# A hybrid encoder layer in half products: new figures in the planner that sets each engine's order

## The chip, the core and the metric

The kernel runs on one core of a Trainium2 chip, in one launch. The metric is the time of that launch on the device, in microseconds (us). Differences here are some tenths of a per cent.

A core has engines that run side by side, each with a queue of its own that it works through in order: TensorE (PE, matmuls; PEld is its loading of weights), VectorE (DVE), ScalarE (ACT), GpSimd (POOL), and SyncE (SP), which here issues all loads and stores. An instruction that needs another engine's result waits for it at the head of its queue, and everything behind it waits too.

## The reference

One layer over 2048 tokens of 1024 features, batch 1, float32:

```python
xn = rms_norm(x, mix_norm_g)
aq, ak, av, mq, mk, mv, mo, i, f, ga, gm = split(xn @ w_in)
A = chunk_band_attention(aq, ak, av, rel_bias)         # 8 heads, chunks of 64, own and 8 before
q, k = split(silu(causal_conv(concat(mq, mk))))
M = sigmoid(mo) * rms_norm(mlstm_chunkwise(q, k, mv, i + b_i, f + b_f))   # 4 heads
y = sigmoid(ga) * (A @ w_att_proj) + sigmoid(gm) * (M @ w_mlstm_proj)
x = x + y @ w_out
x = x + square(relu(rms_norm(x, ffn_norm_g) @ w_up)) @ w_down
out = rms_norm(x, final_norm_g)
```

## The kernel before

**The work.** Each float32 product is made of three matmuls on operands split into a high and a low part (`r` tiles for activations, `wsp` tiles for weights, both float32r; the low part is the value less the high part). ACT casts the high part (L682 for weights, L1651 for activations), DVE subtracts for the low part (L684, L1656, L1658). Large products are blocked 2 by 2 and computed with seven half products in place of eight, so DVE also adds and subtracts blocks before and after. A matmul takes 128x128 weights and 512 columns, into one of eight PSUM banks.

**The stages that matter here.** The layer runs as input projection, attention and mLSTM with further projections (L850) beside them, then from about 1950 us the projections of the mixers' results (`project_quads`, L1255), `w_out`, and the feed-forward part.

- Before `project_quads`, the mixers' results lie in DRAM as `mix0` to `mix3` and `mixa3`. SP loads blocks of them (L1193, L1137, L1138), DVE forms the sums of blocks (L1204, L1140), ACT and DVE split them (L1651, L1656).
- In `project_quads` the weights come as tiles that were split earlier: SP loads them, 1 MB each, from `wsplit29_0` to `wsplit29_6` in DRAM into one of three `wsp` buffers (L587). Each half product fills a bank. ACT copies a bank to an `sc` or `ctx` buffer (L1293), or DVE adds it to such a copy (L1302). Then DVE multiplies by the gate, which SP loaded (L1278), at L1313, and adds the two mixers at L1321.
- Around 1147 and 1208 us, L850's projections go on beside the mLSTM: ACT copies banks (L2286), applies the gates' tanh (L2427) and the convolution's activations (L2458, L2467), DVE the convolution's sums (L2465, L2469) and L2294.

**What sets the order.** The program is first written by some hundred cooperating threads. Then the class `Order` takes all instructions, works out which depends on which (`graph`), and lists them anew for each engine:

- `cost` gives each instruction a duration from its shape, `transfer` one to each DMA, `lag` the delay between an instruction and one that depends on it.
- `due` gives each instruction the time by which it should be done: PE's instructions in the order of the program, summed up; all others backwards from these, less their durations, their lags and, for SP, `FAR`.
- `run` plays the engines forward. On DVE, ACT and SP the instruction with the earliest due time among those whose inputs would be there goes next; on PE the one that comes first in the program. For SP it counts a queue and at most `FLY` = 8 transfers in flight.
- The resulting order on each engine is fixed in the program by dependences without a wait.

So the figures in `Order` decide no duration on the chip, only which instruction stands ahead of which. 12690 matmuls, 3873 DVE, 2458 ACT and 2325 SP instructions are ordered so.

Of the kernel before, what the change touches and what calls it, by code (L numbers as in the profile page):

```python
# [24 lines left out]
F32 = mybir.dt.float32  # L25
# [203 lines left out]
class Order:  # L229
# [1 line left out]

    MARGIN = dict(PE=600.0, Activation=100.0, DVE=100.0, Pool=100.0, SP=2500.0)
    WAKE = dict(PE=43.0, DVE=23.0, Activation=23.0, Pool=69.0, SP=16.0)
    REACH, LAND, FAR, FLY = 1400.0, 1100.0, 2500.0, 8

    def __init__(self, tc):
        self.tc = tc
# [33 lines left out]
    def cost(self, i, e):  # L271
        ins, outs = self.operands(i.ins), self.operands(i.outs)
        n = max(self.count(a) for a in ins + outs)
        bank = any(a.tensor.name.startswith("bank") for a in ins + outs)
        if e == "PE":
            return max(110.0, 13.7 + self.count(outs[0]) / 2.4)
        if e == "SP":
            return 365.0
        if e == "Activation":
            return (75 if bank else 93) + 0.84 * n + (190 if len(outs) > 1 else 0)  # L280
        if e == "Pool":
            return 1200.0 if n <= 8 else 80 + 1.27 * n
        if n <= 4:
            return 155.0
        two = sum(self.count(a) > 4 for a in ins) > 1
        return 60 + (1.13 if two or bank else 0.66) * n + (80 if len(outs) > 1 else 0)

    def transfer(self, i):
        a, b = self.operands((i.outs[0], i.ins[0]))
# [29 lines left out]
    def lag(self, j, k):  # L319
        e, to = self.eng[j], self.eng[k]  # L320
        if e == to != "SP":
            return 0.0
        t = self.WAKE[to] + (0.0 if e == "SP" else 13.0)
        return t + (0.0 if e != "PE" else 175.0 if self.dur[j] >= 140.0 else 130.0)

    def due(self):
# [55 lines left out]
class Layer:  # L382
    LATE, LATE_SPLIT = 3000.0, 2500.0
# [2664 lines left out]
```

## Time and profile before

| what | value |
| --- | --- |
| median of 3 runs | 2767.21 us (2766.9 to 2769.65) |
| the profiled execution, its time | 2767.92 us |
| its span in the profile | 2766.1 us |
| mean granted clock of TensorE | 0.998 |
| DVE, busy | 2100.4 us |
| ACT, busy | 1509.2 us |
| DMA queue of SP | 701.60 MB, 76.6% of 16 engines' span |

The profiled execution's time is 1.8 us more than its span: what lies before the first and behind the last instruction. Each long matmul (128x512) starts 0.227 us behind the one before it, while the trace gives it a duration of about 0.39, since matmuls overlap. Idle time is therefore read from the rows of waits, not from a sum of durations. In a timeline a row is: start, length, engine, line, operation, and in brackets the idle time ahead of it with the instruction that ended it. In the rows names stand without buffer numbers.

### The profile page before, as it was taken

What the parts mean: (1) busy time and instruction counts of PE and PEld (TensorE: products, weight loads), DVE (VectorE), ACT (ScalarE), POOL (GpSimd) and SP (SyncE); (2) the same over time, 40 slices, a digit from 0 to 9 for tenths busy, and PEclk for the clock granted to TensorE, in tenths of its full rate; (3) what the DMA queues carried; (4) which work ended last, traced back from release to release, by engine and by line L of the source; (5) the groups of instructions that cost most, each with busy time, mean ns of one, the idle gap of its engine ahead of it and who ended that gap; (6) DMA issues with size and microseconds to landing.
All of it is one profiled execution on the core that took longest, in us unless ns stands there. A gap on an engine that the chain in (4) does not pass through costs nothing.

```text
span 2766.1 us, 38799 instructions
## 1 busy us (share of the span) xinstructions
PE 2744.5 (99%) x13006; PEld 2282.9 (83%) x13006; DVE 2100.4 (76%) x3873; ACT 1509.2 (55%) x2665; POOL 51.7 (2%) x101
## 2 busy tenths in 40 slices
PE   9999999999999999999999999999999999999999
PEld 7888888888778888777888888888778888888888
DVE  7796799777996866876677788889898755555566
ACT  5664576644454545585456566566335655554444
POOL 0010001000000000000000000000000000000000
PEclk9999999999999999999999999999999999999999
DMA  8968849889756588489899999887967667676564
GB/s 286 286 220 263 238 157 309 299 272 333 265 194 232 196 285 313 136 280 317 293 313 311 308 272 269 263 247 242 330 232 245 216 217 263 236 247 216 195 222 162
DMA packets 339416, 704.08 MB, mean 255 GB/s; under 512 B 37992, under 2 KB 68880, under 8 KB 337424
## 3 DMA queue, kind: packets, MB, share of 16 engines
q1 hardware_dynamic: 339072, 701.60, 76.6%
q8 instruction: 102, 1.67, 0.2%
q14 instruction: 98, 0.80, 0.1%
q10 hardware_dynamic: 144, 0.01, 0.0%
HBM read 483.60 MB, written 217.86 MB: 254 GB/s over the span
## 4 chain that ended last, share of the span: by engine, by line
PE 92%; DVE 4%; DMA 2%; ACT 1%; issue 1%; SPq 0%; DVEq 0%; ACTq 0%
PE bank L850 42%; PE bank L765 11%; PE bank L767 11%; PE bank L766 11%; PE bank L881 3%; PE bank L1842 2%; PE bank L1255 2%; PE bank L1815 2%; PE bank L1873 2%; DVE ctx L2465 1%; DVE wsp L684 1%; PE bank L2128 1%; PE bank L2129 1%; PE bank L2127 1%; PE bank L2113 0%
## 5 line engine op out<-in xcount | busy, mean ns | idle before, releaser
L850 PE MATMUL bank<-r,wsp 128*128 128x512 f32 x5544 | 1268.7, 391 | 6.6 <-ACT ctx L2286 3.3
L850 PEld LDWEIGHTS bank<-r,wsp 128*128 128x128 f32 x5544 | 1039.8, 188 | 227.4 <-ACT ctx L2286 4.7
L684 DVE TENSOR_TENSOR wsp<-wraw,wsp 128x1024 fp32r<-128x1024 f32 x442 | 540.6, 1223 | 347.9 <-ACT wsp L682 338.4
L682 ACT CAST wsp<-wraw 128x1024 fp32r<-128x1024 f32 x442 | 464.9, 1052 | 529.0 <-PE bank L766 211.6
L765 PE MATMUL bank<-r,wsp 128*128 128x512 f32 x1328 | 530.3, 400 | 0.5 <-ACT ctx L2106 0.5
L767 PE MATMUL bank<-r,wsp 128*128 128x512 f32 x1328 | 519.9, 392 | 0.0
L766 PE MATMUL bank<-r,wsp 128*128 128x512 f32 x1328 | 519.4, 391 | 0.0
L767 PEld LDWEIGHTS bank<-r,wsp 128*128 128x128 f32 x1328 | 249.6, 188 | 52.7
L765 PEld LDWEIGHTS bank<-r,wsp 128*128 128x128 f32 x1328 | 249.8, 188 | 46.2 <-ACT ctx L2106 0.9
L766 PEld LDWEIGHTS bank<-r,wsp 128*128 128x128 f32 x1328 | 250.2, 188 | 44.2
L2294 DVE TENSOR_TENSOR ctx<-bank,ctx 128x512 f32<-128x512 f32 x186 | 127.5, 688 | 98.7 <-PE bank L850 96.5
L1656 DVE TENSOR_TENSOR r<-r 128x512 fp32r<-128x512 f32 x251 | 165.6, 687 | 9.6 <-ACT r L1651 9.4
L1651 ACT CAST r<-r 128x512 fp32r<-128x512 f32 x251 | 149.4, 622 | 28.2 <-DMA r<-u 23.5
L2286 ACT COPY ctx<-bank 128x512 f32<-128x512 f32 x186 | 107.7, 582 | 78.7 <-PE bank L850 61.1
L1857 ACT ACTIVATE sc<-sc,scs 128x640 f32<-128x640 f32 (+4 forms) x128 | 97.4, 762 | 67.2 <-DVE scs L1854 61.7
L1878 DVE TENSOR_TENSOR r<-bank,r 128x512 fp32r<-128x512 f32 (+1 forms) x168 | 97.0, 597 | 19.5 <-ACT r L1876 18.9
L1876 ACT CAST r<-bank 128x512 fp32r<-128x512 f32 (+1 forms) x168 | 81.9, 517 | 51.6 <-PE bank L1873 45.9
L1848 DVE CUSTOM_DVE_ANT_0 sc<-bank,bias 128x320 f32<-128x320 f32 (+3 forms) x240 | 103.7, 463 | 5.6 <-PE bank L1842 4.8
L2625 ACT ACTIVATE ctx<-ctx 128x512 f32<-128x512 f32 x96 | 60.5, 630 | 83.6 <-DVE ctx L2294 83.5
L1815 PE MATMUL bank<-r,r 128*128 128x512 f32 x336 | 94.9, 363 | 0.0
L701 DVE TENSOR_TENSOR wraw<-wraw,wraw 128x1024 f32<-128x1024 f32 x76 | 92.7, 1223 | 1.7
L1255 PE MATMUL bank<-r,wsp 128*128 128x512 f32 x336 | 81.0, 403 | 7.3 <-DVE tmp L1313 2.9
(295 smaller groups left out, 2987.3 us busy)
## 6 DMA issues: line engine op xcount, KB each, us to landing
wraw<-in_wf SPq DMA_DIRECT2D x178, 512.0 KB, 4.7
wraw<-wsum SPq DMA_DIRECT2D x136, 512.0 KB, 4.2
r<-u SPq DMA_DIRECT2D x224, 256.0 KB, 3.9
wraw<-in_w SPq DMA_DIRECT2D x71, 512.0 KB, 5.1
ctx<-in_wf SPq DMA_DIRECT2D x128, 256.0 KB, 5.2
u<-ctx SPq DMA_DIRECT2D x128, 256.0 KB, 3.5
wsum<-ctx SPq DMA_DIRECT2D x112, 256.0 KB, 4.4
u<-tmp SPq DMA_DIRECT2D x96, 256.0 KB, 3.9
```

What stands on the lines that cost most here:

```text
L682: nc.scalar.copy(w[:, 0], raw)
L684: nc.vector.tensor_sub(w[:, 1], raw, w[:, 0].bitcast(F32))
L765: mm(ps, lh, rh, start=first, stop=False)
L766: mm(ps, lh, rl, start=False, stop=False)
L767: mm(ps, ll, rh, start=False, stop=last)
L850: mm(ps, wv[:, x, k, n], a[:, y], start=new and k == 0 and x == y == 0, stop=k == 3 and x == 1, skip_group_check=True)
L1255: mm(ps, wv[:, y, x, k, n], a[:, z], start=m < 3 and k == y == z == 0, stop=k == 1 and y == 1, skip_group_check=True)
L1651: self.nc.scalar.copy(dst[:, 0], src)
L1656: self.nc.vector.tensor_sub(dst[:, 1], src, dst[:, 0].bitcast(F32))
L1815: nc.tensor.matmul(acc[:, :, c0:c0 + w], st, sl[:, :, o:o + w], start=n == 0, stop=n == total - 1)
L2286: nc.scalar.copy(t[:, o:o + 512], ps)
L2294: nc.vector.tensor_add(t[:, o:o + 512], ps, t[:, o:o + 512])
```

## The change

The change gives `Order` other figures. No instruction is added or left out, and nothing is computed differently.

- A column or a further input counts by the number of inputs: ACT is 92 ns longer for each input beside the first, DVE 62 ns longer with more than two (before: ACT 190 and DVE 80 where there was a second output).
- A matmul on plain float32 that isn't a transpose counts double.
- An instruction that depends on the one before it on the same engine waits `AGAIN` ns (before: 0); results of ACT and DVE reach other engines `LATE` ns later.
- `FAR`, by which SP's transfers are due ahead of their use, goes from 2500 to 5000 ns.

```diff
-    REACH, LAND, FAR, FLY = 1400.0, 1100.0, 2500.0, 8
+    AGAIN = dict(PE=0.0, Activation=125.0, DVE=85.0, Pool=60.0)
+    LATE = dict(PE=0.0, Activation=98.0, DVE=50.0, Pool=0.0)
+    REACH, LAND, FAR, FLY = 1400.0, 1100.0, 5000.0, 8
...
         if e == "PE":
-            return max(110.0, 13.7 + self.count(outs[0]) / 2.4)
+            plain = ins[0].dtype == F32 and not i.is_transpose
+            return max(110.0, 13.7 + self.count(outs[0]) / 2.4) * (2.0 if plain else 1.0)
...
-            return (75 if bank else 93) + 0.84 * n + (190 if len(outs) > 1 else 0)
+            return (75 if bank else 93) + 0.84 * n + 92 * (len(ins) - 1)
...
-        return 60 + (1.13 if two or bank else 0.66) * n + (80 if len(outs) > 1 else 0)
+        return 60 + (1.13 if two or bank else 0.66) * n + (62 if len(ins) > 2 else 0)
...
         if e == to != "SP":
-            return 0.0
-        t = self.WAKE[to] + (0.0 if e == "SP" else 13.0)
+            return self.AGAIN[e]
+        t = self.WAKE[to] + (0.0 if e == "SP" else 13.0 + self.LATE[e])
```

In the new order 707 of the 12690 matmuls stand in another place (by at most 24), 2430 of DVE's 3873 instructions, 982 of ACT's 2458 and 1254 of SP's 2325. From here on, lines of code behind the changed ones have numbers that are 3 higher in the changed kernel (L1313 is L1316); the text uses those of before.

Three places are shown, in the order of before and then of the changed kernel.

**DVE at about 2004 to 2017 us, in `project_quads`.** L1313 multiplies a bank, or its copy in `sc`, by the gate; L1302 adds a bank to a copy. The instruction on `tmp2_108` and `sc3_104` frees `sc3`, which ACT's next copy (L1293) of bank 6 writes. Before:

```order
L1313 SCALAR_TENSOR_TENSOR ctx3_115<-ctx3_115,bank5_133 128x512
L1302 TENSOR_TENSOR sc0_98<-bank2_130,sc0_98 128x512
L1313 SCALAR_TENSOR_TENSOR ctx4_116<-ctx4_116,sc0_98 128x512
L1313 SCALAR_TENSOR_TENSOR tmp5_111<-tmp5_111,bank1_129 128x512
L1321 TENSOR_TENSOR ctx1_113<-ctx1_113,tmp5_111 128x512
L1302 TENSOR_TENSOR sc2_102<-bank5_133,sc2_102 128x512
L1313 SCALAR_TENSOR_TENSOR ctx15_127<-ctx15_127,sc2_102 128x512
L1302 TENSOR_TENSOR sc1_100<-bank1_129,sc1_100 128x512
L1313 SCALAR_TENSOR_TENSOR tmp4_110<-tmp4_110,sc1_100 128x512
L1313 SCALAR_TENSOR_TENSOR tmp2_108<-tmp2_108,sc3_104 128x512
```

and in the changed kernel:

```order
L1316 SCALAR_TENSOR_TENSOR ctx3_115<-ctx3_115,bank5_133 128x512
L1316 SCALAR_TENSOR_TENSOR tmp2_108<-tmp2_108,sc3_104 128x512
L1324 TENSOR_TENSOR ctx13_125<-ctx13_125,tmp2_108 128x512
L1316 SCALAR_TENSOR_TENSOR tmp5_111<-tmp5_111,bank1_129 128x512
L1324 TENSOR_TENSOR ctx1_113<-ctx1_113,tmp5_111 128x512
L1305 TENSOR_TENSOR sc0_98<-bank2_130,sc0_98 128x512
L1316 SCALAR_TENSOR_TENSOR ctx4_116<-ctx4_116,sc0_98 128x512
```

The instruction on `tmp2` and the sum behind it moved eight places up, to directly behind the one on `ctx3`. On PE, the six matmuls into bank 6 that wait for the copy moved 23 places up, ahead of three groups of six and five more matmuls. A second instruction on `tmp2`, later in this stretch, moved six places up.

**SP at about 1965 to 1977 us, ahead of `project_quads`.** Here `mix2`, `mix3` and `mixa3` are the mixers' results, `gate2` and `gate3` the gates, `wsplit29` the weights, and `fin` a store. Before:

```order
L587 DMA wsp2_63<-wsplit29_1 128x2048
L1278 DMA ctx10_122<-gate2 128x512
L1193 DMA tmp3_109<-mix2 128x512
L1193 DMA tmp4_110<-mix3 128x512
L2547 DMA fin0<-ctx9_121 128x512
L2547 DMA fin1<-ctx0_112 128x512
L587 DMA wsp0_61<-wsplit29_0 128x2048
L1193 DMA ctx6_118<-mix3 128x512
L1137 DMA tmp2_108<-mixa3 64x512
L1138 DMA tmp5_111<-mixa3 64x512
L1193 DMA tmp0_106<-mix3 128x512
```

and in the changed kernel:

```order
L1196 DMA tmp3_109<-mix2 128x512
L1196 DMA tmp4_110<-mix3 128x512
L2550 DMA fin0<-ctx9_121 128x512
L644 DMA wraw1_65<-in_wf 128x1024
L1196 DMA ctx6_118<-mix3 128x512
L1140 DMA tmp2_108<-mixa3 64x512
L1141 DMA tmp5_111<-mixa3 64x512
L1196 DMA tmp0_106<-mix3 128x512
L590 DMA wsp2_63<-wsplit29_1 128x2048
L1281 DMA ctx10_122<-gate2 128x512
```

The loads of `mix` and `mixa` and one store now stand ahead of both weight loads; `wsplit29_1` and the load of `gate2` moved seven places down, as did `wsplit29_0`, which now stands six rows behind `wsplit29_1`. On DVE, the sums of these blocks (L1204) and what follows from them moved ahead of the bank sums of L1302 by 11 or 12 places.

**ACT at about 1142 to 1148 us.** L2286 copies bank 6 to `ctx8`; L2427 works on a result of DVE. Before:

```order
L682 CAST wsp1_62<-wraw3_67 128x1024
L2286 COPY ctx2_114<-bank2_130 128x512
L2458 ACTIVATE ctx0_112<-ctx15_127,cvw_143 128x512
L2427 ACTIVATE ctx12_124<-ctx12_124 128x512
L2286 COPY ctx8_120<-bank6_134 128x512
L2467 ACTIVATE ctx15_127<-ctx0_112 128x512
L682 CAST wsp2_63<-wraw0_64 128x1024
```

and in the changed kernel:

```order
L2289 COPY ctx8_120<-bank6_134 128x512
L2430 ACTIVATE ctx12_124<-ctx12_124 128x512
L685 CAST wsp2_63<-wraw0_64 128x1024
L2470 ACTIVATE ctx15_127<-ctx0_112 128x512
L2430 ACTIVATE ctx10_122<-ctx10_122 128x512
```

The copy of bank 6 moved ahead of the activation on `ctx12`; the weights' cast moved ahead of L2467.

## The prediction

> **What bounds the kernel now.** I read the page's busy times first, then what TensorE waited for, then the windows of 100 us to place these waits. All rows are of the one profiled execution; times are us.
>
> ```profile
> PE 2744.5 (99%) x13006; PEld 2282.9 (83%) x13006; DVE 2100.4 (76%) x3873; ACT 1509.2 (55%) x2665; POOL 51.7 (2%) x101
> PE 92%; DVE 4%; DMA 2%; ACT 1%; issue 1%; SPq 0%; DVEq 0%; ACTq 0%
> ```
>
> TensorE is busy for 2744.5 of a span of 2766.1 and carries 92% of the chain that ended last. The change removes no matmul, so only the 21.6 us in which PE is not busy, and whatever makes matmuls longer, can move. About 1.0 of the 21.6 is the start (the row of L441 below, which stays). The rows of PE's waits say what else there is (waited for, total us, times, longest):
>
> ```profile
> PE bank L850 <- ACT ctx L2286: 3.3, 2, 1.9
> PE bank L1255 <- DVE tmp L1313: 2.9, 2, 2.1
> PE bank L1255 <- ACT r L1651: 2.0, 1, 2.0
> PE bank L1255 <- ACT sc L1293: 1.9, 1, 1.9
> PE bank L850 <- ACT r L1651: 1.7, 1, 1.7
> PE bank L850 <- DVE r L1658: 1.1, 2, 0.5
> PE bank L441 <- DVE ones L438: 1.0, 1, 1.0
> PE bank L1972 <- DVE cum L1968: 0.6, 2, 0.3
> ```
>
> The five largest rows add up to 11.8 us, in seven waits. Two stretches hold most of them, 1900 to 2100, where DVE is busy for 89% (columns: length, then busy time of PE, PEld, DVE, ACT, POOL, granted clock of PE, DMA share, GB/s):
>
> ```profile
> 1200.00:1300.00 100.00, 96.72 (x421) 78.34 (x420) 73.11 (x96) 61.49 (x93) 0.00 (x0) 1.00 0.90 313
> 1900.00:2000.00 100.00, 97.44 (x451) 80.62 (x450) 89.12 (x170) 48.86 (x88) 0.00 (x0) 0.98 0.83 276
> 2000.00:2100.00 100.00, 95.28 (x411) 77.78 (x410) 89.30 (x135) 34.46 (x54) 0.00 (x0) 0.98 0.68 236
> ```
>
> The clock of 0.98 in these two rows is a second cost. Behind some stalls PE runs at half clock:
>
> ```profile
> 1148.40:1151.80 3.40, 3.40 (x9) 2.67 (x9) 1.85 (x3) 1.74 (x4) 0.00 (x0) 0.51 0.62 224
> 1991.60:1995.00 3.40, 3.40 (x8) 2.72 (x9) 3.40 (x6) 1.17 (x2) 0.00 (x0) 0.51 0.76 309
> 2015.40:2018.80 3.40, 3.40 (x10) 2.63 (x9) 2.57 (x4) 0.00 (x0) 0.00 (x0) 0.51 0.56 113
> 2023.10:2026.50 3.40, 3.40 (x15) 2.81 (x16) 3.30 (x6) 0.39 (x1) 0.00 (x0) 1.00 0.75 214
> ```
>
> The last row is the same length at full clock: 15 matmuls, or 3.40 / 15 = 0.227 each. The other three did 9, 8 and 10, so the dips cost 6, 7 and 5 matmuls: 1.4, 1.6 and 1.1 us.
>
> The TensorE page of the Trainium skill ("TensorE: Matmul & The Clock Gate", section "What's actually happening") says that the clock is halved after at least one idle window of about 3.4 us. The trace disagrees on the length, since no wait above is over 2.1 us and three are followed by a dip. Taken strictly, the rule would give these dips a cause other than the stalls; that is the third rival.
>
> **The change part by part.** Nothing is computed differently; the tables order each engine's instructions anew. So no duration changes, and a term is a wait that goes or comes. I give no price to the tables themselves. I compare the two orders at each stall, and take the times from the trace of before.
>
> *A. The quads' later columns (2004 to 2026).* PE's rows, with the idle time in brackets, then DVE's and ACT's:
>
> ```profile
> 2010.05 2.79 PE L1255 MATMUL bank<-r,wsp 128*128 128x512 f32 x11 [0.75 <-DVE tmp L1313]
> 2014.70 6.23 PE L1255 MATMUL bank<-r,wsp 128*128 128x512 f32 x19 [1.86 <-ACT sc L1293]
> 2023.04 3.26 PE L1255 MATMUL bank<-r,wsp 128*128 128x512 f32 x13 [2.11 <-DVE tmp L1313]
> ```
> ```profile
> 2005.26 0.69 DVE L1313 SCALAR_TENSOR_TENSOR ctx<-ctx,bank 128x512 f32<-128x512 f32 x1 [0.67 <-PE bank L1255]
> 2007.98 0.69 DVE L1302 TENSOR_TENSOR sc<-bank,sc 128x512 f32<-128x512 f32 x1 [2.03 <-PE bank L1255]
> 2012.68 1.29 DVE L1313 SCALAR_TENSOR_TENSOR tmp<-tmp,sc 128x512 f32<-128x512 f32 x2
> 2022.30 0.68 DVE L1313 SCALAR_TENSOR_TENSOR tmp<-tmp,bank 128x512 f32<-128x512 f32 x1
> 2014.07 0.58 ACT L1293 COPY sc<-bank 128x512 f32<-128x512 f32 x1 [10.93 <-DVE tmp L1313]
> ```
>
> DVE's second instruction at 2012.68 (2013.3) frees the buffer that ACT's copy at 2014.07 needs, and the copy frees the bank that PE waits for until 2014.70. It stands behind eight instructions, of which the first waits 2.03 for PE. In the new order it is directly behind the one at 2005.26, where DVE is idle until 2007.98. It would end near 2006.9, and the copy 0.6 later, near 2007.5. The instruction of 2010.05's wait then ends by 2008.4, before PE asks at 2009.3 (2010.05 - 0.75). The one at 2022.30, for which PE waits 2.11, moves 6 up, 6 x 0.65 = 3.9 us. So the three waits go: 0.75 + 1.86 + 2.11 + the dip of 1.1 = 5.8. What is late next is the copy again: PE's group behind it is moved up too, by 23 matmuls, and asks at about 2006.6 (2009.3 less the two groups of six that it now precedes, 12 x 0.227 = 2.7). It would wait some 1.1 there, with the time to wake: 5.8 - 1.1, **-4.7** (bounds: 0 and -5.8).
>
> *B. The quads' first column (1965 to 1995).*
>
> ```profile
> 1990.28 0.73 PE L1255 MATMUL bank<-r,wsp 128*128 128x512 f32 x2 [2.02 <-ACT r L1651]
> 1991.56 2.93 PE L1255 MATMUL bank<-r,wsp 128*128 128x512 f32 x6 [0.54 <-DVE r L1656]
> 1981.04 2.14 DVE L1204 TENSOR_TENSOR ctx<-ctx,ctx 128x512 f32<-128x512 f32 x3 [3.59 <-DMA ctx<-mix]
> 1970.99 0.46 SPq L1193 DMA_DIRECT2D ctx<-mix  x1
> ```
>
> DVE stands idle for 3.59 until a load of mix that was issued at 1970.99 lands, and the queue that forms behind it reaches PE at 1990. The new order issues the mix loads ahead of two 1 MB and one 0.26 MB transfers. If they land early enough, 2.02 + 0.54 + the dip of 1.6 = 4.2 goes. Two things come in its place. The weights wsplit29_1 now stand behind them:
>
> ```profile
> 1965.18 0.44 SPq L587 DMA_DIRECT2D wsp<-wsplit  x1
> DMA to landing us min/median/max: 8.3/8.3/8.3
> L1255 PE MATMUL bank<-r,wsp x10: 389/390/390, 1975.9 to 1977.9; 128*128 128x512 f32 x10
> 1973.00:1981.00 8.00, 8.00 (x37) 6.64 (x36) 2.08 (x3) 2.38 (x4) 0.00 (x0) 1.00 1.05 355
> SPq L1137 <- DMA wsp<-wsplit: 2.0, 1, 2.0
> ```
>
> Issued at 1965.18, they landed 8.3 later, at 1973.5; PE reads them first at 1975.9, a slack of 2.4. Moved ahead of them are five transfers of 128x512 f32 (0.262 MB) and two of 64x512 (0.131), 1.57 MB, which at 355 GB/s is 4.4 us, so PE would stall for 2.0. Lower bound: 0, if the queue is shorter by then. Upper bound: the last row shows SP held until a transfer eight places earlier landed; eight places ahead of the weights is now a mix load, issued near 1966.4, and if the weights' issue is held to 1973, the landing is at 1981.3, a stall of 5.4 and a dip of 1.6. I take 2.0, the figure nearest to the rows. Second, DVE now does about 20 instructions, of 0.65 each by the rows in A, 13 us, between that mix sum and the bank sum for which PE's group at 1986.7 waits. With PE 2.0 later, the sum may start no later than about 1975.7. Before, it started at 1981.04, 10.05 after the load's issue, since both weight tiles and a gate tile stood ahead of that load; without these 2.36 MB, 6.6 us at 355 GB/s, it could start near 1974.4. The margin is 1.3, so I count no stall there, and each us by which the load lands later than 1975.7 costs one. B: -4.2 + 2.0 = **-2.2** (bounds: -4.2 and +7).
>
> *C. 1147.* ACT's rows, and PE's:
>
> ```profile
> 1143.01 0.82 ACT L2458 ACTIVATE ctx<-ctx,cvw 128x512 f32<-128x512 f32 x1
> 1146.04 0.63 ACT L2427 ACTIVATE ctx<-ctx 128x512 f32<-128x512 f32 x1 [2.20 <-DVE ctx L2294]
> 1146.58 0.57 ACT L2286 COPY ctx<-bank 128x512 f32<-128x512 f32 x1
> 1147.19 3.17 PE L850 MATMUL bank<-r,wsp 128*128 128x512 f32 x9 [1.89 <-ACT ctx L2286]
> ```
>
> The copy that PE waits for stands behind an activation that itself waits 2.20 for DVE. The new order swaps the two. The copy can run in that gap, done by 1144.4, before PE's 1145.3. The wait of 1.89 and the dip of 1.4 go: **-3.2**. What waits for the activation loses the copy's 0.57 at most, and not even that if the copy fits in the gap. Bounds: 0 (if the copy's buffer is free no earlier) and -3.3.
>
> *D. Smaller ones.* The cast behind the 1.7 of L850 <- ACT L1651 moves seven places up on ACT. At about 0.6 each, with two longer ones, more than the wait; I count half, **-0.9** (0 to -1.7). The matmuls that wait for L1968 twice, 0.6, move 10 places later: **-0.4**. The second wait of L2286 (3.3 - 1.9 = 1.4) is left in the same order, as is L1658's 1.1. Both stay.
>
> *E. New small stalls.* 707 matmuls, 2430 DVE, 982 ACT and 1254 SP instructions stand elsewhere by up to tens of places, and the trace cannot show where one now waits in front of the others. Bounds: 0, and 15, as many as the old order had altogether by its waits. I put 2 for the attention stretch, where loads that PE's transposes wait for are moved back, 1 for the L1658 chain, which one longer instruction now precedes, and 1 for the rest: **+4**.
>
> The sum: -4.7 - 2.2 - 3.2 - 0.9 - 0.4 + 4 = -7.4. The profiled execution took 2767.92, 1.8 more than its span; 2767.9 - 7.4 = 2760.5. It stands 0.7 above the median of the runs, 2767.21, so by that median the forecast is **2759.8**.
>
> **The rivals.**
> 1. *The stalls change places.* A and C come off at half, since a queue that is ordered anew puts another instruction in front: -4.0 - 2.2 - 0.6 + 4 = -2.8, or 2764.4. For it: every large wait here is a head of a queue that waits, and there are thousands of moved ones. Against it: in A and C the engine was idle while the wanted instruction was ready.
> 2. *Slower: the loads' lead starves the weights.* All of SP's transfers are due 2.5 us earlier, so activations overtake 1 MB weight loads as in B. The page's row of GB/s, in 40 slices of 69 us, has eight at over 300:
>
> ```profile
> GB/s 286 286 220 263 238 157 309 299 272 333 265 194 232 196 285 313 136 280 317 293 313 311 308 272 269 263 247 242 330 232 245 216 217 263 236 247 216 195 222 162
> ```
>
>    If a weight load slips by 4.4 us against a slack of 2.4 in each, that is 8 x 2.0 = 16 us, and three dips of 1.4: -11.4 (the sum without E) + 16 + 4.2 = +8.8, or 2776. It decides from 5.5 + 11.4 = 16.9 us of new stalls. Against it: of the moved weight loads, I found PE's slack overrun only in B.
> 3. *The dips have another cause and stay.* Then 4.1 (1.1 + 1.6 + 1.4) of the gains is lost: -3.3, or 2763.9. Against it: each of the three dips begins right behind a stall. (It is what the Trainium skill's rule on the clock, above, would give.)
> 4. *Everything goes and nothing comes:* 5.8 + 4.2 + 3.3 + 1.7 + 0.6 = 15.6 less, 2751.6.
>
> **How the numbers follow.** A measurement of this kernel can tell 0.2%, 5.5 us, from no change: faster is below 2761.7, slower above 2772.7. Forecast 0.46, of which 0.39 below 2761.7 and 0.07 above; stalls change places 0.25; dips stay 0.04; everything goes 0.10; slower 0.15. Faster: 0.39 + 0.10 = 0.49; same: 0.07 + 0.25 + 0.04 = 0.36; slower 0.15. The range takes in rival 4, 2751, and reaches up to 2773, so that it leaves out little more than the slower case.
>
> **What would show it.** In the profile after, PE's waits should have no row of L1313 or L1293 near 2010 to 2023, none of L2286 near 1147, and windows at clock 1.00 there; a new wait of PE for wsplit should stand near 1976, below 3 us. Waits of PE for wsp in other stretches would speak for rival 2, a list of many waits of about 1 us for rival 1. The prediction is wrong if PE's waits sum to more than before, or if it is the first column that stalls for more than 6 us.

## The result and the profile after

| | before | changed |
| --- | --- | --- |
| median of 4 runs | 2767.62 us (2766.9 to 2769.65) | 2754.18 us (2752.87 to 2757.34) |
| ratio | | 0.9952, 95% interval 0.9935 to 0.9969 |
| the profiled execution | 2767.92 us | 2757.34 us |

The changed kernel is faster by 0.48%, 13.4 us by the medians. The forecast was 2759.8, and 2751 to 2773 as the range. The profiled execution of the changed kernel is the slowest of its four, so its profile shows only 10.6 us of the gain. Where one execution is explained, the sum goes against 10.6; how this differs from the medians comes up below.

The first rows of the page, busy time by engine and the chain that ended last:

```profile
PE 2739.9 (99%) x13006; PEld 2280.4 (83%) x13006; DVE 2069.5 (75%) x3873; ACT 1509.4 (55%) x2665; POOL 52.9 (2%) x101
PE 97%; DMA 1%; DVE 1%; ACT 0%; issue 0%; SPq 0%; POOL 0%; ACTq 0%
```

The span is 2755.5, so PE is not busy for 15.6 us, against 21.6 before; the rest of the gain, 4.6, is busy time, of which a part was matmuls at half clock. DVE's share of the chain went from 4% to 1%. What PE waited for in the changed kernel (total us, times, longest; lines are 3 higher than before):

```profile
PE bank L853 <- ACT ctx L2289: 3.5, 1, 3.5
PE bank L2105 <- DMA r<-mfar: 2.1, 2, 1.8
PE bank L853 <- ACT r L1656: 1.3, 1, 1.3
PE bank L444 <- DVE ones L441: 1.0, 1, 1.0
PE bank L1553 <- POOL r_far L1585: 0.7, 1, 0.7
PE bank L1258 <- ACT sc L1296: 0.7, 1, 0.7
PE bank L853 <- DVE r L1659: 0.5, 1, 0.5
```

The rows of `project_quads` (L1255, now L1258) that held 6.8 us before (2.9, 2.0 and 1.9) have shrunk to one wait of 0.7. The waits on top are others: 3.5 at 1262, where 1.4 stood before, and 1.8 of the row of `mfar`, a load, at 460. The windows of 100 us (length, busy time and count of matmuls, then as before):

```profile
700.00:800.00 100.00, 97.98 (x423) 79.95 (x422) 95.88 (x138) 46.66 (x67) 0.00 (x0) 0.98 0.63 214
1100.00:1200.00 100.00, 100.00 (x443) 82.82 (x442) 86.06 (x119) 66.97 (x102) 0.00 (x0) 1.00 0.54 176
1200.00:1300.00 100.00, 96.06 (x415) 78.52 (x415) 71.12 (x95) 59.40 (x90) 0.00 (x0) 0.98 0.89 308
1900.00:2000.00 100.00, 99.91 (x469) 82.78 (x468) 87.61 (x167) 49.13 (x87) 0.00 (x0) 1.00 0.86 295
2000.00:2100.00 100.00, 99.31 (x439) 81.91 (x438) 88.98 (x135) 36.24 (x54) 0.00 (x0) 1.00 0.72 246
```

Two of these stretches as they were before:

```profile
1100.00:1200.00 100.00, 98.11 (x426) 80.73 (x426) 84.54 (x116) 62.10 (x94) 0.00 (x0) 0.98 0.50 165
700.00:800.00 100.00, 98.86 (x431) 80.40 (x431) 98.27 (x139) 47.80 (x69) 0.00 (x0) 1.00 0.66 221
```

Where all matmuls are long ones, their count is the best gauge, since it holds idle time and half clock alike: a stretch without loss has 443, and each one missing is 0.227 us. From 2000 to 2100 it went from 411 to 439 (7.3 us lost, now 0.9), from 1100 to 1200 it is full, for 426, from 1200 to 1300 it fell from 421 to 415, and from 700 to 800 from 431 to 423. The clock of 0.98 in these last two is half clock that was not there before (1.00).

### The profile page after: what moved, and what is told of

Read it like the earlier page. It is cut to its first block, busy times and chain, and to the rows that moved or that the text cites. A ratio compares the mean times of both kernels' runs of the same rounds, so it can differ in the third digit from the quotient of the medians.

```text
span 2755.5 us, 38840 instructions
## 1 busy us (share of the span) xinstructions
PE 2739.9 (99%) x13006; PEld 2280.4 (83%) x13006; DVE 2069.5 (75%) x3873; ACT 1509.4 (55%) x2665; POOL 52.9 (2%) x101
## 4 chain that ended last, share of the span: by engine, by line
PE 97%; DMA 1%; DVE 1%; ACT 0%; issue 0%; SPq 0%; POOL 0%; ACTq 0%
PE bank L853 45%; PE bank L768 12%; PE bank L770 12%; PE bank L769 12%; PE bank L884 3%; PE bank L1258 3%; PE bank L1845 2%; PE bank L1818 2%; PE bank L1876 2%; PE bank L2131 0%; PE bank L2132 0%; PE bank L2116 0%; PE bank L2130 0%; DMA r<-mfar 0%; PE bank L935 0%; DMA tmp<-mixa 0%
## 5 line engine op out<-in xcount | busy, mean ns | idle before, releaser
L853 PE MATMUL bank<-r,wsp 128*128 128x512 f32 x5544 | 1268.1, 390 | 6.0 <-ACT ctx L2289 3.5
L768 PE MATMUL bank<-r,wsp 128*128 128x512 f32 x1328 | 529.2, 399 | 0.0
L769 PE MATMUL bank<-r,wsp 128*128 128x512 f32 x1328 | 519.1, 391 | 0.0
L770 PE MATMUL bank<-r,wsp 128*128 128x512 f32 x1328 | 518.6, 391 | 0.0
L2289 ACT COPY ctx<-bank 128x512 f32<-128x512 f32 x186 | 107.8, 582 | 90.6 <-PE bank L853 73.9
L1845 PE MATMUL bank<-r,r 128*128 128x320 f32 (+3 forms) x480 | 85.5, 305 | 0.0
```

Source lines behind the costliest of these rows:

```text
L768: mm(ps, lh, rh, start=first, stop=False)
L769: mm(ps, lh, rl, start=False, stop=False)
L770: mm(ps, ll, rh, start=False, stop=last)
L853: mm(ps, wv[:, x, k, n], a[:, y], start=new and k == 0 and x == y == 0, stop=k == 3 and x == 1, skip_group_check=True)
L1845: nc.tensor.matmul(bks[x][:, :w], q[:, y, i * P:(i + 1) * P], kf[:, f * P + x * w:f * P + x * w + w], start=y == 0, stop=y == 1)
L2289: nc.scalar.copy(t[:, o:o + 512], ps)
```

## The experiments

Two theories were set against each other. **Theory 1:** the gain is local. It is the waits that go at three places, 1147, 1975 to 1995 and 2004 to 2026, less new waits elsewhere; each can be had by itself. **Theory 2:** the gain belongs to the order as a whole, because truer delays, or more time for loads, let everything run earlier. Each run's ratio is to before, timed beside it.

### The order of one kernel in a stretch of the other

Both orders are worked out from the same list of instructions. All instructions that the order of before starts ahead of a given matmul are kept in the order of the first kernel, those behind it in the order of the second. Since whatever an instruction depends on starts ahead of it, the result is again a valid order.

```diff
-        Order(self.tc).run()
+        splice(self.tc, [(None, False), (9058, True), (9712, False)])
...
+    cut = [0.0 if c is None else began[ob["PE"][c]] for c, _ in pieces[1:]]
+    part = [sum(t >= c for c in cut) for t in began]
+    for e in ob:
+        for p, (_, new) in enumerate(pieces):
+            out[e] += [k for k in (oa if new else ob)[e] if part[k] == p]
```

The numbers are matmuls; 9058 to 9712 is 1940 to 2100 us of before. `True` stands for the changed order. In these kernels the lines lie further down (L1258 of the changed kernel is L1306).

**s_quads**, as in the diff:

> The order of the changed kernel only from 1940 to 2100 us of before (the quads), the order of before everywhere else. Theory 1 (the gain is local: the waits of PE at 1990 to 2023 and their dips are gone there, and nothing else pays for it): PE's lost time in this stretch falls from 12.7 to about 2.4 us, so 10.3 us less, 2757 (2755 to 2759). Theory 2 (the gain needs the new order of the whole program, because loads and queues run earlier everywhere): less than half of it, 2763 or more.

Measured: 2757.16 (2755.23 to 2760.22), ratio 0.9969 (0.9958 to 0.9981). Theory 1. What PE waited for includes a row that the changed kernel did not have:

```profile
PE bank L1306 <- DMA wsp<-wsplit: 2.1, 1, 2.1
...
PE bank L1306 <- ACT sc L1344: 0.7, 1, 0.7
```

They were issued by SP at 1968.28:

```profile
1968.28 0.33 SPq L638 DMA_DIRECT2D wsp<-wsplit  x1
```

This is the stall on the weights that the prediction put at 2.0, with the same order of instructions in this stretch as in the changed kernel, where it did not come. More on it below.

**s_rest**, the opposite: `[(None, True), (9058, False), (9712, True)]`.

> The other way round: the order of the changed kernel everywhere but from 1940 to 2100 us, where the order of before stands. Theory 1: the waits at 1990 to 2023 come back, about 10 us over the changed kernel, 2764 (2761 to 2767); the rest of the change gives only what it gains at 1147 and loses at 460, 713 and 1262. Theory 2: at most 5 us over the changed kernel, 2759 or less.

Measured: 2764.53 (2762.65 to 2765.71), ratio 0.9992 (0.9983 to 1.0001). Theory 1: without the quads' stretch the change is worth some 2 us, and the interval does not tell even that from nothing. The gains of the two halves, 9.7 (2766.84 - 2757.16) and 2.3, add up to 12.0, nearly the 13.4 of the whole.

**s_c**, the changed order from 1135 to 1160 us only: `[(None, False), (5241, True), (5334, False)]`.

> The order of the changed kernel only from 1135 to 1160 us, where ACT's copy of bank 6 stands ahead of the activation that waits for DVE. Theory 1: PE's wait of 1.89 at 1147 and the half clock behind it (1.4 us) go, 3.3 us less, 2764.3 (2763.5 to 2765.5), and the clock of that stretch is 1.00. Theory 2 (the stall moves to a later place): within 1 us of before, 2767.

Measured: 2764.00 (2762.28 to 2765.97), ratio 0.9991 (0.9982 to 1.0000), 2.8 us. The window shows why:

```profile
1100.00:1200.00 100.00, 99.88 (x441) 82.11 (x439) 85.96 (x118) 65.73 (x100) 0.00 (x0) 1.00 0.54 177
```

441 matmuls for the 426 before are 15 x 0.227 = 3.4 us, and the clock is 1.00. Theory 1; by the times alone it would not be shown, since the interval reaches 1.

**s_best**, the order of before where the changed kernel had new waits: `[(None, False), (5086, True), (5653, False), (5930, True)]`.

> The order of before up to 1100 us and from 1235 to 1300 us, the order of the changed kernel elsewhere. In the changed kernel's profile PE's waits at 460 and 494 (1.8 and 0.7), at 713 and at 1262 (3.5, with a dip) are new or longer than before. Theory 1 (local): they are gone here, about 5 us under the changed kernel, 2749 (2747 to 2752). Theory 2 (such waits are the price of the earlier work elsewhere, or come by chance of an execution): within 2 us of the changed kernel, 2753 to 2756.

Measured: 2750.30 (2749.84 to 2752.06), ratio 0.9944 (0.9932 to 0.9957). Theory 1.

### One part of the change at a time

**e_costs:** durations alone.

```diff
-            return max(110.0, 13.7 + self.count(outs[0]) / 2.4)
+            plain = ins[0].dtype == F32 and not i.is_transpose
+            return max(110.0, 13.7 + self.count(outs[0]) / 2.4) * (2.0 if plain else 1.0)
...
-            return (75 if bank else 93) + 0.84 * n + (190 if len(outs) > 1 else 0)
+            return (75 if bank else 93) + 0.84 * n + 92 * (len(ins) - 1)
...
-        return 60 + (1.13 if two or bank else 0.66) * n + (80 if len(outs) > 1 else 0)
+        return 60 + (1.13 if two or bank else 0.66) * n + (62 if len(ins) > 2 else 0)
```

> Before with the durations' part of the change alone (inputs count on ACT and DVE, plain float32 matmuls count double; FAR, AGAIN and LATE as before). Its order has all three moves: the mix loads ahead of the weights, tmp2 up in the quads, the copy ahead of the activation at 1147. Theory 1 (the gain is these three moves, whichever figure makes them): about 10.3 + 3.3 less, and unknown losses of up to 5 elsewhere, 2757 (2752 to 2760). Theory 2 (more time for loads carries it): 2763 or more.

Measured: 2756.95 (2755.59 to 2759.11), ratio 0.9966 (0.9954 to 0.9978).

**e_far:** `FAR` = 5000 alone.

> Before with FAR = 5000 alone. Its order has the move at 1147, but the weights still stand ahead of the mix loads by four places and tmp2 still stands nine places down. Theory 1: 3.3 less than before, 2764 (2761 to 2767). Theory 2: most of the gain, 2758 or less.

Measured: 2764.57 (2763.41 to 2766.39), ratio 0.9994 (0.9985 to 1.0002).

**e_lags:** `AGAIN` and `LATE` alone.

> Before with AGAIN and LATE alone. Its order has none of the three moves. Theory 1: as before, 2767 (2763 to 2770). Theory 2 (truer delays between instructions carry it): 2760 or less.

Measured: 2767.78 (2765.79 to 2771.49), ratio 1.0006 (0.9997 to 1.0014).

**e_nofar:** the changed kernel with `FAR` back.

```diff
-    REACH, LAND, FAR, FLY = 1400.0, 1100.0, 5000.0, 8
+    REACH, LAND, FAR, FLY = 1400.0, 1100.0, 2500.0, 8
```

> The changed kernel with FAR back at 2500. Its order has all three moves. Theory 1: as the changed kernel, 2755 (2751 to 2759). Theory 2 (more time for loads carries it): at least 5 over the changed kernel, 2760 or more.

Measured: 2751.61 (2749.89 to 2752.26), ratio 0.9945 (0.9933 to 0.9957).

All four times came out where theory 1 put them, but the three moves account only for e_costs and e_nofar. e_far has the move at 1147, and the wait of 1.89 is gone, yet PE waits for the next copy 3.5 us later, which stands behind an activation that waits for DVE; PE's row, then ACT's:

```profile
1150.67 5.55 PE L850 MATMUL bank<-r,wsp 128*128 128x512 f32 x23 [1.39 <-ACT ctx L2286]
```
```profile
1148.03 0.63 ACT L2467 ACTIVATE ctx<-ctx 128x512 f32<-128x512 f32 x1 [2.40 <-DVE ctx L2465]
```

In its profiled execution the clock is 1.00 in all three stretches that were at 0.98 before, though waits of 2.17 and 2.11 stand in the quads. e_lags has none of the three moves, and PE (L852 is L850 here) has no wait at 1147 all the same:

```profile
1141.64 14.67 PE L852 MATMUL bank<-r,wsp 128*128 128x512 f32 x64
```

It pays for this with new waits at 452 and 498 (1.7 and 2.8) and with 3.5 in place of 1.4 at 1267. So in these two the time agrees with theory 1 partly by luck. More time for loads is not needed for the gain: without it the kernel is no slower. Whether it costs something (the changed kernel's ratio of 0.9952 against 0.9945) the intervals leave open. The delays by themselves made no gain in time.

### One wait taken off the head of a queue

PE's longest wait left in s_best, 1.44 at 1257, is for a copy on ACT that stands behind a cast of weights, and the cast comes late; in e_nofar, where the same pair stands, it waits for PE. **f_swap** exchanges these two and nothing else:

```diff
+    acts.remove(copy)
+    acts.insert(acts.index(cast), copy)
```

> s_best with one pair of ACT instructions exchanged: at 1255 the copy of bank 5 goes ahead of the cast of weights that waits for PE. Theory 1 (a wait is the head of a queue that waits, and taking it off the head takes the whole wait): PE's wait of 1.44 for L2337 at 1257 goes, 1.6 less than s_best, 2748.7 (2747.5 to 2750). Theory 2 (the copy is late by what it needs itself, or PE stalls at the next group instead): as s_best, with a wait of similar size within 10 us of the place.

Measured: 2750.33 (2749.70 to 2752.68), ratio 0.9942 (0.9930 to 0.9955), against 2750.25 for s_best beside it. A miss: theory 2. PE's and then ACT's timeline (start, length, what, idle time ahead of it):

```profile
1259.66 4.61 PE L910 MATMUL bank<-r,wsp 128*128 128x512 f32 x19 [1.88 <-ACT ctx L2346]
```
```profile
1254.12 0.58 ACT L2346 COPY ctx<-bank 128x512 f32<-128x512 f32 x1 [3.18 <-DMA wsum<-ctx]
1254.90 1.05 ACT L742 CAST wsp<-wraw 128x1024 fp32r<-128x1024 f32 x1 [0.20 <-PE bank L910]
1257.84 0.63 ACT L2685 ACTIVATE ctx<-ctx 128x512 f32<-128x512 f32 x1 [1.89 <-DVE ctx L2354]
1258.50 0.63 ACT L2689 ACTIVATE ctx<-ctx 128x512 f32<-128x512 f32 x1
1259.04 1.05 ACT L2346 COPY ctx<-bank 128x512 f32<-128x512 f32 x2
```

The copy now runs at 1254.12 and its wait is gone. But the next copy, at 1259.04, stands behind an activation that waits 1.89 for DVE, and PE waits 1.88 for it. In s_best the wait of 1.44 had covered this one: PE went on behind it for 9.60 us without another.

**f_nofar_swap** exchanges the same pair in e_nofar:

> The changed kernel with FAR back at 2500 (e_nofar) and the same pair exchanged. Theory 1: the wait of 1.39 at 1255 goes, 1.5 less than e_nofar, 2750 (2748.5 to 2751.5). Theory 2: as e_nofar, 2751.6.

Measured: 2752.46 (2751.76 to 2754.47), ratio 0.9948 (0.9934 to 0.9962). Here the wait at 1255 did go, and one of 0.4 is left there, but the kernel is no faster than e_nofar, 2751.61, by the ratios. Its profiled execution is the slowest of the five, 2754.47. The first row of PE's waits says what came there instead, in the quads, where not one instruction is ordered differently from e_nofar; whether the other four executions had it is not shown:

```profile
PE bank L1315 <- DMA wsp<-wsplit: 2.9, 2, 2.5
```

In e_nofar's profile PE has no wait for these weights. The rows of SP at which they were issued, in e_nofar and then here:

```profile
1958.86 0.33 SPq L590 DMA_DIRECT2D wsp<-wsplit  x1
```
```profile
1959.94 0.33 SPq L647 DMA_DIRECT2D wsp<-wsplit  x1
```

The same order stalled for nothing in one execution and for 2.5 in the other. The weights were issued 1.1 us later, while PE came to them 0.5 us earlier (1967.40 and 1966.95):

```profile
1967.40 4.83 PE L1258 MATMUL bank<-r,wsp 128*128 128x512 f32 x20
```
```profile
1969.44 3.18 PE L1315 MATMUL bank<-r,wsp 128*128 128x512 f32 x7 [2.49 <-DMA wsp<-wsplit]
```

### Run again beside them

> s_best once more, beside the kernels compared with it: 2750.3 (2749 to 2752).

Measured: 2750.25 (2750.10 to 2751.44), ratio 0.9941 (0.9928 to 0.9953).

> The changed kernel once more. Local theory: 2754 (2752 to 2757), about 4 over r_best by its waits at 460, 494, 713 and 1262. If its waits there come by chance of one execution, it is within 2 of r_best, and the new profile has none of them.

Measured: 2753.09 (2751.04 to 2756.70), ratio 0.9951 (0.9938 to 0.9963). On the same chip s_best is 2.8 us faster by the medians, less than the 4 expected. Its waits are on both sides of the two theories: the new profile has 3.3 at 1258, 1.3 at 711 and 0.7 at 492 again, so these belong to the order; it has none for `mfar` at 460, so that one came with one execution.

## Why the prediction was right, and where it was off

The direction and the range held, and the place of the gain was the one forecast. The size was low: 13.4 by the medians for a sum of 7.4. In the changed kernel's profiled execution, term by term:

| term | forecast | measured | from |
| --- | --- | --- | --- |
| A, 2000 to 2100 | -4.7 | -6.4 | 28 more matmuls x 0.227 |
| B, 1900 to 2000 | -2.2 | -4.1 | idle 2.56 to 0.09, and the dip, 1.7 |
| C, 1100 to 1200 | -3.2 | -3.9 | 17 more matmuls x 0.227 |
| D and E, the rest | +2.7 | +3.8 | 10.6 less the three above |

- **A was right in its mechanism, step by step.** The copy that PE waits for was expected to stay late by 1.1 behind a load and the instruction on `tmp2`. It is the one wait left there, ACT's copy first and PE's row behind it:

```profile
2002.59 0.58 ACT L1296 COPY sc<-bank 128x512 f32<-128x512 f32 x1 [4.87 <-PE bank L1258]
```
```profile
2003.23 2.11 PE L1258 MATMUL bank<-r,wsp 128*128 128x512 f32 x8 [0.69 <-ACT sc L1296]
```

   The size was 0.69. What was mis-sized is the dip. The prediction took 1.1 from 10 matmuls against 15, but such a row counts every matmul that touches its stretch, also the one under way at its start. The prediction's row of 2014.70 shows it better: 19 matmuls took 6.23, where 18 x 0.227 + 0.39 = 4.5 would do, so the dip cost 1.7. The clock column says the same, (1 - 0.51) x 3.40 = 1.7. With this, idle time and dip account for 5.7 of the 6.4 (4.72 - 0.69 + 1.7). Another 0.3 is in the way idle time is told: a matmul's 0.39 ends 0.16 behind the earliest start of the next, 0.227, so each wait costs 0.16 more than its row says, and three went for one that came. The last 0.4 is open.

- **C was right.** s_c shows it alone: 2.8 by the times and 3.4 by the profile, for -3.2. (Its terms, 1.89 and 1.4, add up to 3.3, and with the dip at 1.7 to 3.6.)

- **B failed at one step: "I take 2.0, the figure nearest to the rows"** for the weights behind the mix loads. In the changed kernel there was no such stall. SP's rows, and PE's loading of the first weights of the quads:

```profile
1963.98 0.38 SPq L1196 DMA_DIRECT2D ctx<-mix  x1
...
1967.27 0.33 SPq L590 DMA_DIRECT2D wsp<-wsplit  x1
```
```profile
L1258 PEld LDWEIGHTS bank<-r,wsp x18: 187/188/189, 1976.0 to 1979.8; 128*128 128x128 f32 x18
...
  DMA wsp<-wsplit: 0.4, 1
```

   I moved the weights' landing by what 1.57 MB take, 4.4. But the mix loads went out up to 7.0 us earlier than before (1963.98 for 1970.99), the weights were issued only 2.1 later (1967.27 for 1965.18), and they were there at 1976.0, as PE came to them. The bound that held their issue until 1973 was far off. The mechanism is real: s_quads stalled for 2.1 with the same order, having issued the weights at 1968.28, and f_nofar_swap for 2.5. What differs is how long before PE comes the weights are issued, and how long they take. In the changed kernel and in e_nofar PE came 8.8 and 8.5 us behind the issue and found them just there: the loading of weights had waited 0.4 us in both. In s_quads and f_nofar_swap PE came 7.2 and 7.0 behind it and could go on only 9.3 and 9.5 behind it; the row of s_quads:

```profile
1977.53 2.81 PE L1306 MATMUL bank<-r,wsp 128*128 128x512 f32 x11 [2.06 <-DMA wsp<-wsplit]
```

   The forecast had one figure for what is in these profiles either 0 or 2 to 2.5. That an execution alone decides between them is not shown: the two profiles of the changed kernel have no such stall, nor have the two of s_best.

   The other step of B, whether the mix loads land before 1975.7, came out well inside: DVE began the sums at 1971.95, after an idle time of 0.64 in place of 3.59.

```profile
1971.95 2.14 DVE L1207 TENSOR_TENSOR ctx<-ctx,ctx 128x512 f32<-128x512 f32 x3 [0.64 <-DMA ctx<-mix]
```

- **D held in part.** The wait of L850 for L1651 (1.7) is gone, with one of 0.5 at 1220 in its place, and L1968's 0.6 left the list. But "the second wait of L2286 is left in the same order" missed that DVE's order had changed around it: it grew from 1.4 to 3.5. The copy stands behind a sum on DVE that stands behind weights; DVE's rows, then ACT's:

```profile
1259.21 1.23 DVE L687 TENSOR_TENSOR wsp<-wraw,wsp 128x1024 fp32r<-128x1024 f32 x1 [1.59 <-ACT wsp L685]
1260.36 0.68 DVE L575 TENSOR_TENSOR ctx<-ctx,ctx 128x512 f32<-128x512 f32 x1
```
```profile
1261.11 0.58 ACT L2289 COPY ctx<-bank 128x512 f32<-128x512 f32 x1 [1.93 <-DVE ctx L575]
```

- **E, put at +4, was about right for the profiled execution by luck.** That execution holds two half-clock stretches and a load that the repeated one has not, as the last section shows, together 5.2. By the medians D and E are together +1.0 (13.4 less the 14.4 of A, B and C), for +2.7 forecast. What lasts of E has its largest part at 1262; s_best, which takes the new waits out by the order of before, is 2.8 to 3.9 us under the changed kernel. So the forecast of 2759.8 is 5.6 above the median because A, B and C gave 4.3 more than forecast and D and E took 1.7 less, 6.0 in all, while the median of before is 0.4 above the one that the forecast started from. A, B and C are each read from one execution of either kernel.

- **Rival 1**, that stalls change places, is true on a small scale: at 1262 in the changed kernel, and at 1260 in f_swap, where it took the whole gain. **Rival 2** has its stall on weights, but at one place and not in eight. **Rival 3**, that the half clock has another cause, fell in part: with the waits of A, B and C their dips went too. But a wait does not always bring one, as the last section shows.

## What to carry to other kernels

When an engine's order is set by a planner, look at the few places where the engine that bounds the kernel waits, and read there which instruction stands ahead of the wanted one; the times of all runs came within 4 us of the sum of the places that could be foreseen, though in e_far and e_lags other places made up the sum. A wait that is removed has its own worth only if no other was hidden by it: read what is next in line on the same queue, and on the queue that feeds it. And where two orders win in different stretches, splice them; that tells where a gain sits, and here gave the fastest kernel, 2750.3.

## What the runs showed of the hardware that was not expected

The prediction priced each half-clock stretch behind a wait as certain. It is not. The same wait, for the instruction on `tmp2` in the order of before, 2.11 us long in both, was followed by 15 matmuls in 3.40 us in before (the row of 2023.10 in the prediction) and by 8 in s_rest:

```profile
2017.20:2020.60 3.40, 3.40 (x8) 2.64 (x9) 3.02 (x5) 0.00 (x0) 0.00 (x0) 0.52 0.61 205
```

The longest wait, for L2289, 3.46 and 3.34 us, shows the same in two executions of the changed kernel, the first and the repeated one:

```profile
1261.80:1265.20 3.40, 3.40 (x9) 2.67 (x10) 1.30 (x2) 1.96 (x4) 0.00 (x0) 0.54 0.92 302
```
```profile
1257.90:1261.30 3.40, 3.40 (x15) 2.81 (x16) 1.28 (x2) 1.99 (x4) 0.00 (x0) 1.00 0.87 298
```

Six or seven matmuls, 1.4 to 1.6 us, hang on it each time. The waits at 713 and 711 (1.29 and 1.27, each with one of 0.41 behind it) were followed by half clock in the first execution and not in the repeated one:

```profile
715.40:718.80 3.40, 3.40 (x10) 2.63 (x9) 3.40 (x7) 2.88 (x4) 0.00 (x0) 0.50 1.05 389
```
```profile
713.00:716.40 3.40, 3.40 (x15) 2.43 (x14) 3.40 (x7) 2.79 (x4) 0.00 (x0) 1.00 1.02 368
```

These two half-clock stretches, 1.7 each by the clock, and the load of `mfar`, 1.8, are 5.2 of the 5.5 us between these two executions of one kernel (2757.34 and 2751.85). The Trainium skill ("TensorE: Matmul & The Clock Gate", section "What's actually happening") says that the activity is counted in windows of about 3.4 us that run freely. The traces fit this, in that equal waits differ in what follows; the windows themselves no run here shows. They do not fit the idle time of a whole window that the page asks for, since a wait of 1.89 was enough at 1147.
